# First feed-forward product in token-major form, seven products for eight in two of its k pairs

## The chip, the cores and the metric

The kernel runs on one core of a Trainium2 chip. The metric is device time in microseconds, from three timed runs; one further execution was taken with the hardware profiler, and all rows come from that one.

## What is computed

One decoder layer for 256 tokens of width 2048, all in float32. The change concerns the second half, the gated feed-forward block:

```python
x = layer_norm(ALPHA * x + merged @ w_o, ln1_g, ln1_b)
gate_f, up = split(x @ w_ffn_in, 2)            # 2048 -> 2 x 5632
f = (silu(gate_f) * up) @ w_ffn_out            # 5632 -> 2048
x = layer_norm(ALPHA * x + f, ln2_g, ln2_b)
```

Ahead of it stand the combined input projection with attention, a gated spatial mixing and a state-space layer (S5), which the change only touches at two small places.

## The kernel before

**Precision.** Every weight and activation is cut into a high part (float32r, by a copy on ScalarE) and a low part (the remainder, by a subtraction on VectorE). A product is high x high + high x low + low x high.

**Units.** All weights stream through units of up to 128 x 1024 elements (512 KB). A unit is loaded on SP's DMA queue into one of four raw buffers (`raw`), copied (`split_h`, line 263), subtracted (`split_l`, line 269) into one of four pairs `wh`, `wl`, and consumed by TensorE. The order on every engine is the program's own: the loop over the units calls `advance` (copies for units up to three ahead, as long as fewer than four pairs are live; loads as long as a raw buffer is free), emits the unit's matmuls, one step of each spawned task (generators that `yield` between units), the unit's `post`, deferred work (`later`), and then `remainders` (the subtractions, each followed by the next load).

**First product (`wide`).** An item is one 128-column tile of the gate or of the up matrix, k = 2048, in two units of eight k tiles. The weights are stationary, the activations move: line 80 takes the high weights over 512 columns (256 tokens high, 256 low), line 81 the low weights over the 256 high columns. The two halves of the PSUM bank are added in `sum_halves`; a gate tile becomes tanh(x/2), an up tile completes silu(gate) x up, and `copy_split` writes the high and low part of the feature-major h tile. There are 88 items; the first four run through `quad_tiles`, the others one after another.

**Second product (`tall`).** Token-major: activations stationary, weights moving with 512 columns, three matmuls per k tile and token half (lines 166 to 168). Its first unit's `before`, `ln2_load`, loads the second norm's weights into the buffer of the activations `x1T`.

**Residual.** `z` (256 x 2048, the first norm's result in rows) stays in SBUF, in the buffer with the tag t16, from the first norm to the end.

**S5.** `s5_setup` and `tables` are tasks in the first 60 us or so; GpSimd then runs a recurrence of 128 steps (lines 547 to 550), whose result TensorE reads in `s5_out` (line 561).

## Time and profile before

| | |
|---|---|
| time, median of 3 runs | 1589.97 us (1588.33 to 1590.55) |
| profiled execution, own time | 1590.49 us |
| its span, first to last instruction | 1588.7 us |
| TensorE busy | 1566.2 us, 99% |
| VectorE / ScalarE / GpSimd busy | 59% / 48% / 35% |
| DMA | 307.5 MB, 194 GB/s |

A busy time counts an instruction from start to end, and matmuls overlap: a matmul is busy for longer than the distance to the next one (its pitch). Costs on TensorE are therefore read as distances between starts.

### The profile page before, as it was taken

The numbers are of one execution on the slowest core, as the hardware profiler recorded it, in microseconds if no ns is written. First come the engines' busy times: TensorE is split into PE (matmuls) and PEld (weight loads), VectorE is DVE, ScalarE is ACT, GpSimd is POOL, SyncE is SP. The second block draws the span as 40 slices with busy tenths as digits, with TensorE's granted clock in tenths as the row PEclk, the third lists the DMA queues.
The fourth block names the chain that finished last, engine by engine and source line by source line (L and its number), as shares of the span: only waits on it lengthen the run. The fifth ranks groups of instructions, "written<-read, shape, count | busy, mean of one in ns | idle before, by whom it ended". The sixth has DMA issues, their size and how long they took to land.

```text
span 1588.7 us, 24112 instructions
## 1 busy us (share of the span) xinstructions
PE 1566.2 (99%) x9094; PEld 1359.8 (86%) x9094; DVE 931.2 (59%) x1232; ACT 762.9 (48%) x1040; POOL 557.8 (35%) x1147
## 2 busy tenths in 40 slices
PE   8999999999999999999999999999999999999996
PEld 6888888998889998889789888888888888888885
DVE  5545555656755665469667555555555555455455
ACT  5444444556544444465444545454545444443342
POOL 7469999944999999103011000000000000000002
PEclk9999999999999999999999999999999999999998
DMA  8575566665656555557863555555555556666663
GB/s 276 178 249 187 190 210 191 181 179 175 214 185 197 183 185 194 178 161 207 296 225 121 190 192 182 190 184 188 184 188 184 187 186 232 218 191 195 195 191 105
DMA packets 106492, 307.50 MB, mean 194 GB/s; under 512 B 27567, under 2 KB 28079, under 8 KB 106120
## 3 DMA queue, kind: packets, MB, share of 16 engines
q1 hardware_dynamic: 106280, 305.82, 60.0%
q8 instruction: 71, 1.16, 0.3%
q14 instruction: 45, 0.37, 0.1%
q0 software_dynamic: 96, 0.15, 0.0%
HBM read 303.78 MB, written 5.53 MB: 195 GB/s over the span
## 4 chain that ended last, share of the span: by engine, by line
PE 94%; DVE 3%; DMA 1%; ACT 1%; issue 1%; POOL 0%; SPq 0%; POOLq 0%; ACTq 0%
PE ps_mm L80 40%; PE ps_mm L81 20%; PE ps_mm L166 9%; PE ps_mm L167 9%; PE ps_mm L168 9%; DVE wl L269 2%; PE ps_mm L868 1%; PE ps_mm L867 1%; PE ps_mm L866 1%; PE ps_sd L525 1%; PE ps_mm L109 0%; PE ps_mm L112 0%; PE ps_sd L670 0%; DMA raw<-in_w_o_dram 0%; PE ps_sd L719 0%
## 5 line engine op out<-in xcount | busy, mean ns | idle before, releaser
L269 DVE TENSOR_TENSOR wl<-raw,wh 128x1024 fp32r<-128x1024 f32 (+1 forms) x544 | 654.3, 1227 | 157.5 <-ACT wh L263 156.8
L263 ACT ACTIVATE wh<-raw 128x1024 fp32r<-128x1024 f32 (+1 forms) x544 | 556.7, 1024 | 371.0 <-PE ps_mm L168 169.1
L80 PE MATMUL ps_mm<-xT,wh 128*128 128x512 f32 x1344 | 482.6, 402 | 7.5 <-ACT wh L59 5.5
L80 PE MATMUL ps_mm<-x1T,wh 128*128 128x512 f32 x1344 | 474.9, 399 | 0.0
L81 PE MATMUL ps_mm<-xT,wl 128*128 128x256 f32 x1344 | 379.8, 283 | 0.4 <-DVE wl L269 0.4
L81 PE MATMUL ps_mm<-x1T,wl 128*128 128x256 f32 x1344 | 378.0, 281 | 0.0
L80 PEld LDWEIGHTS ps_mm<-xT,wh 128*128 128x128 f32 x1344 | 254.7, 190 | 69.5 <-ACT wh L59 5.5
L80 PEld LDWEIGHTS ps_mm<-x1T,wh 128*128 128x128 f32 x1344 | 252.9, 188 | 62.7
L947 POOL TENSOR_TENSOR z<-z,ln2w 128x512 f32<-128x512 f32 (+1 forms) x4 | 5.2, 1302 | 726.6 <-ACT z L946 726.6
L81 PEld LDWEIGHTS ps_mm<-xT,wl 128*128 128x128 f32 x1344 | 256.8, 191 | 1.2 <-DVE wl L269 0.7
L81 PEld LDWEIGHTS ps_mm<-x1T,wl 128*128 128x128 f32 x1344 | 254.5, 189 | 0.0
L547 POOL TENSOR_TENSOR t<-s5keep,X 128x48 f32<-128x48 f32 x254 | 132.3, 521 | 44.2 <-ACT X L529 24.4
L550 POOL TENSOR_TENSOR X<-X,t 128x48 f32<-128x48 f32 x255 | 129.0, 506 | 20.0
L167 PE MATMUL ps_mm<-wl,h 128*128 128x512 f32 x340 | 132.5, 390 | 0.0
L166 PE MATMUL ps_mm<-wh,h 128*128 128x512 f32 x340 | 132.4, 390 | 0.0
L168 PE MATMUL ps_mm<-wh,h 128*128 128x512 f32 x340 | 132.4, 390 | 0.0
L549 POOL TENSOR_TENSOR X<-X,t 128x48 f32<-128x48 f32 x255 | 115.0, 451 | 40.5 <-ACT X L529 40.5
L1047 DVE TENSOR_TENSOR tmp<-ps_mm,tmp 128x256 f32<-128x256 f32 x88 | 37.4, 425 | 153.1 <-ACT tmp L1046 153.1
L548 POOL TENSOR_TENSOR t<-s5keep,X 128x48 f32<-128x48 f32 x254 | 116.4, 458 | 0.0
L318 ACT ACTIVATE tmp<-ps_mm,bcol 128x256 f32<-128x256 f32 x90 | 42.6, 473 | 136.7 <-PE ps_mm L81 136.5
L1046 ACT ACTIVATE tmp<-ps_mm 128x256 f32<-128x256 f32 x88 | 33.6, 382 | 152.0 <-PE ps_mm L81 152.0
L166 PEld LDWEIGHTS ps_mm<-wh,h 128*128 128x128 f32 x340 | 63.9, 188 | 13.3
(214 smaller groups left out, 1758.2 us busy)
## 6 DMA issues: line engine op xcount, KB each, us to landing
raw<-in_w_f_dram SPq DMA_DIRECT2D x264, 512.0 KB, 4.1
raw<-in_w_b_dram SPq DMA_DIRECT2D x164, 512.0 KB, 4.7
raw<-in_w_o_dram SPq DMA_DIRECT2D x32, 512.0 KB, 5.1
raw<-in_w_v_dram SPq DMA_DIRECT2D x24, 512.0 KB, 4.0
raw<-in_w_p_dram SPq DMA_DIRECT2D x32, 384.0 KB, 3.6
raw<-in_w_zv_dram SPq DMA_DIRECT2D x16, 384.0 KB, 3.7
tmp<-tab SPq DMA_DIRECT2D x64, 64.0 KB, 2.8
raw<-in_w_p_dram SPq DMA_DIRECT2D x16, 256.0 KB, 2.9
```

The costliest lines, as they stand in the source:

```text
L80: T.matmul(ps, lhsT=h[:, j * 128:(j + 1) * 128], rhs=a, start=k == 0, stop=last, skip_group_check=True)
L81: T.matmul(ps[:, 0:256], lhsT=l[:, j * 128:(j + 1) * 128], rhs=a[:, 0:256], start=False, stop=last, skip_group_check=True)
L166: T.matmul(ps[:, :n], lhsT=ah, rhs=hs, start=k == 0, stop=False)
L167: T.matmul(ps[:, :n], lhsT=ah, rhs=ls, start=False, stop=False)
L168: T.matmul(ps[:, :n], lhsT=al, rhs=hs, start=False, stop=k == total - 1)
L263: A.activation(h[:, :m], raws[n][:, :m], AF.Copy)
L269: V.tensor_tensor(l[:, :m], raws.pop(n)[:, :m], h[:, :m].bitcast(F32), op=ALU.subtract)
L318: A.activation(t, ps[:, 256:512], AF.Identity, bias=bcol[:, col:col + 1], scale=scale)
L547: G.tensor_tensor(t1, keep[:, 0], prev, op=ALU.mult)
L548: G.tensor_tensor(t2, keep[:, 1], prev[:, :, ::-1], op=ALU.mult)
L549: G.tensor_tensor(cur, cur, t1, op=ALU.add)
L550: G.tensor_tensor(cur, cur, t2, op=ALU.add)
```

## The change

For ten groups of four column tiles (all but the first group) the first product is now token-major: the activations are stationary and 512 weight columns (four tiles side by side) move. A unit is one pair of k tiles for the four gate tiles or the four up tiles, loaded as 512 runs of 1 KB where it was 128 runs of 4 KB. A group has eight k pairs. In six of them a gate and an up unit each take 12 matmuls (`mk8`). In the pairs 3 and 5 the 2 x 2 blocks (two token halves, two k tiles; two k tiles, gate and up) are multiplied with seven products for eight: `combine` forms sums of weights on VectorE before the split, four units `g`, `u`, `t1`, `tt` take 6, 6, 3 and 6 matmuls, and the sums of activations `S` are formed once (`sums`). Eight PSUM banks hold a group; `evict`, `gates_` and `ups` add them up, and `turns` transposes the gated product into the feature-major h tiles, during the group behind.

`S` lies in the buffer t16; so `first_sums` writes the residual rows to DRAM (GpSimd's queue) and `ln2_load` reads them back. In the early part, `s5_setup` waits three units longer before its transposes, and `tables` pauses after each of its four blocks.

```diff
+    PAIRS = (3, 5)
+    SP = len(PAIRS)
+    FIRST, LAST = 1, 10
...
         def load(n):
             u = units[n]
+            if u.role in ("t1", "tt"):
+                return
             r = raw_tile()
-            nc.sync.dma_start(r[:, :u.k * u.n], u.src)
+            if u.role:
+                u.pair[u.role] = r
+            dst = r[:, :u.k * u.n]
+            nc.sync.dma_start(dst if len(u.src.shape) == 2 else dst.rearrange("p (f c) -> p f c", f=u.src.shape[1]),
+                              u.src)
             raws[n] = r
...
+            if u.role == "g" and "t" not in u.pair:
+                combine(u.pair)
+            elif u.role == "t1":
+                raws[n] = u.pair["t"][:, 0:512]
+            elif u.role == "tt":
+                raws[n] = u.pair["t"][:, 512:1536]
             A.activation(h[:, :m], raws[n][:, :m], AF.Copy)
             hl[n] = rest[n] = (h, l)
 
+        def combine(p):
+
+
+            p["t"] = s6([128, 1536], F32, "tt")
+            b = [p[e][:, 0:1024].rearrange("p (f k c) -> p k f c", f=4, k=2) for e in "gu"]
+            b11, b21, b12, b22 = b[0][:, 0], b[0][:, 1], b[1][:, 0], b[1][:, 1]
+            t1, t2, t4 = (p["t"][:, 512 * i:512 * i + 512].rearrange("p (f c) -> p f c", f=4) for i in range(3))
+            V.tensor_tensor(t1, b12, b11, op=ALU.subtract)
+            V.tensor_tensor(b12, b22, b12, op=ALU.subtract)
+            V.tensor_tensor(t2, b12, b11, op=ALU.add)
+            V.tensor_tensor(t4, b21, t2, op=ALU.subtract)
+
         def split_l(n):
-            m = units[n].k * units[n].n
+            u = units[n]
+            m = u.k * u.n
             h, l = rest.pop(n)
             V.tensor_tensor(l[:, :m], raws.pop(n)[:, :m], h[:, :m].bitcast(F32), op=ALU.subtract)
+            if u.role not in ("t1", "tt"):
+                pos["raw"] -= 1
+            if u.role is None and u.pair and "u" in u.pair:
+                combine(u.pair)
 
...
-            for _ in range(5):
+            for _ in range(8):
...
                 else:
                     V.tensor_copy(tb2, ps[0:8, 0:127])
+                yield
...
+        def first_sums():
+
+            big["zd"] = dram.tile([128, 2, D], F32, name="zd")
+            for t in range(2):
+                nc.gpsimd.dma_start(big["zd"][:, t, :], big["z"][:, t, :])
+            spawn(sums())
...
+            xr = s6([128, 4, 256], F32, "xr")
+            for i, e in enumerate(PAIRS):
+                x = big["x1T"][:, 2 * e:2 * e + 2, :].bitcast(F32)
+                V.tensor_tensor(xr[:, 2 * i:2 * i + 2], x[:, :, 0:256], x[:, :, 256:512], op=ALU.add)
...
+            V.tensor_tensor(sr[:, 0], a21, a22, op=ALU.add)
+            V.tensor_tensor(sr[:, 1], sr[:, 0], a11, op=ALU.subtract)
+            V.tensor_tensor(sr[:, 2], a11, a21, op=ALU.subtract)
+            V.tensor_tensor(sr[:, 3], a12, sr[:, 1], op=ALU.subtract)
...
+            big["S"] = sb.tile([128, 4, SP, 256], F32R, tag="t16", bufs=1, name="S")
+            for s in range(4):
+                o = big["S"][:, s]
+                copy_split(o[:, :, 0:128], o[:, :, 128:256], sr[:, s])
...
+        def three(ps, a, h, l, start, stop):
+            T.matmul(ps, lhsT=a[0], rhs=h, start=start, stop=False)
+            T.matmul(ps, lhsT=a[1], rhs=h, start=False, stop=False)
+            T.matmul(ps, lhsT=a[0], rhs=l, start=False, stop=stop)
...
+            def cols(w, j):
+                return w.rearrange("p (f k c) -> p k f c", f=4, k=2)[:, j]
+
+            def prod(n, a, h, l, start, stop):
+                if n not in P:
+                    P[n] = bank(tags[n in (1, 5, 6, 7)])
+                three(P[n], a, h, l, start, stop)
...
+            def mk(role, i):
+                def mm(h, l):
+                    z = 2 * PAIRS[i]
+                    ends = i == 0, i == SP - 1
+                    if role == "g":
+                        prod(1, act2(0, z), cols(h, 0), cols(l, 0), *ends)
+                        prod(2, act2(0, z + 1), cols(h, 1), cols(l, 1), False, False)
+                    elif role == "u":
+                        prod(7, act_s(2, i), cols(h, 0), cols(l, 0), *ends)
+                        prod(3, act_s(3, i), cols(h, 1), cols(l, 1), False, False)
+                    elif role == "t1":
+                        prod(5, act_s(0, i), h[:, 0:512], l[:, 0:512], *ends)
+                    else:
+                        prod(6, act_s(1, i), h[:, 0:512], l[:, 0:512], *ends)
+                        prod(4, act2(1, z + 1), h[:, 512:1024], l[:, 512:1024], False, False)
+                return mm
+
+            def mk8(up, i):
+                def mm(h, l):
+                    for t in range(2):
+                        for j in range(2):
+                            prod(((2, 4), (3, 8))[up][t], act2(t, 2 * i + j), cols(h, j), cols(l, j),
+                                 (i, j) == (0, 0), (i, j) == (7, 1))
+                return mm
...
+            def begin():
+                if g > FIRST:
+                    spawn(turns(g - 1))
+
+            def evict():
+                c = P["c"] = {n: tmp() for n in (1, 7, 6, 5)}
+                A.activation(c[1], P[1], AF.Copy)
+                V.tensor_tensor(c[6], P[6], c[1], op=ALU.add)
+                V.tensor_tensor(c[7], P[7], c[6], op=ALU.add)
+                V.tensor_tensor(c[6], P[5], c[6], op=ALU.add)
+                V.tensor_tensor(c[5], P[5], c[7], op=ALU.add)
+
+            def gates_():
+                c = P["c"]
+                P["w"] = [tmp(), tmp()]
+                for t, (n, m) in enumerate(((1, 2), (7, 4))):
+                    V.tensor_tensor(c[n], P[m], c[n], op=ALU.add)
+                    A.activation(P["w"][t], c[n], AF.Tanh, scale=0.5)
...
+            def ups():
+                c = P["c"]
+                for n, m in ((6, 3), (5, 8)):
+                    V.tensor_tensor(c[n], P[m], c[n], op=ALU.add)
+
+                def rest(t):
+                    w, a, b = P["w"][t], c[(1, 7)[t]], c[(6, 5)[t]]
+                    V.scalar_tensor_tensor(w, w, 1.0, a, op0=ALU.add, op1=ALU.mult)
+                    V.tensor_tensor(w, w, b, op=ALU.mult)
+                    if t == 0:
+                        later(lambda: rest(1), 0)
+                later(lambda: rest(0), 0)
+                big["w", g] = P["w"]
...
+            src = [d["w_f1"][8 * g + up:8 * g + 8:2].rearrange("f p k c -> p f k c") for up in range(2)]
...
+            for i in range(8):
+                s = [a[:, :, 2 * i:2 * i + 2, :].rearrange("p f k c -> p f (k c)") for a in src]
+                if i in PAIRS:
+                    e = PAIRS.index(i)
+                    pair = pairs[e]
+                    units.append(Unit(s[0], 8, 128, mk("g", e), role="g", pair=pair))
+                    units.append(Unit(s[1], 8, 128, mk("u", e), role="u", pair=pair))
+                    units.append(Unit(None, 4, 128, mk("t1", e), role="t1", pair=pair))
+                    units.append(Unit(None, 8, 128, mk("tt", e), role="tt", pair=pair,
+                                      post=evict if e == SP - 1 else None))
+                else:
+                    units.append(Unit(s[0], 8, 128, mk8(0, i), post=gates_ if i == 7 else None,
+                                      before=begin if i == 0 else None))
+                    units.append(Unit(s[1], 8, 128, mk8(1, i), post=ups if i == 7 else None,
+                                      pair=pairs[PAIRS.index(i + 1)] if i + 1 in PAIRS else None))
...
+        def turns(g):
+
+            tag = "mm" if (LAST - g) % 2 else "sd"
+            for _ in range(3):
+                yield
+            for t in range(2):
+                ps = bank(tag)
+                for f in range(4):
+                    T.transpose(ps[:, f * 128:(f + 1) * 128], big["w", g][t][:, f * 128:(f + 1) * 128], ident)
+                f = 4 * g
+                while f < 4 * g + 4:
+                    n = min(4 * g + 4, 12 if f < 12 else f + 3 - f % 3) - f
+                    h_tile(f)
+                    y = big["h0"][:, f:f + n] if f < 12 else big["h", (f - 12) // 3][:, f % 3:f % 3 + n]
+                    copy_split(y[:, :, t * 128:(t + 1) * 128], y[:, :, 256 + t * 128:256 + (t + 1) * 128],
+                               ps.rearrange("p (f c) -> p f c", f=4)[:, f - 4 * g:f - 4 * g + n], 0.5)
+                    f += n
+                yield
...
+            big["z"] = sb.tile([128, 2, D], F32, tag="t16", bufs=1, name="z")
+            for t in range(2):
+                nc.sync.dma_start(big["z"][:, t, :], big["zd"][:, t, :])
             w = sb.tile([128, 2, D], F32, tag="t32", bufs=1, name="ln2w")
+            spawn(turns(LAST))
             for i, nm in enumerate(("ln2_g", "ln2_b")):
                 nc.sync.dma_start(w[:, i, :], d[nm].partition_broadcast(128))
...
+            if 4 <= i < 8 * FIRST:
+                wide(srcs, 8, act_x1, post, before=first_sums if i == 4 else None)
+        for g in range(FIRST, LAST + 1):
+            seven(g)
+        for i, (srcs, post) in enumerate(f1):
+            if i >= 8 * LAST + 8:
```

TensorE in the first product. Before, the end of one item's tile and the start of the next (each half-item's `wh` serves eight such pairs):

```order
L80 MATMUL ps_mm_10333<-x1T_8812,wh_10279 128x512
L81 MATMUL ps_mm_10333<-x1T_8812,wl_10280 128x256
L80 MATMUL ps_mm_10384<-x1T_8812,wh_10302 128x512 [waits Activation_49]
L81 MATMUL ps_mm_10384<-x1T_8812,wl_10303 128x256 [waits DVE_49]
L80 MATMUL ps_mm_10384<-x1T_8812,wh_10302 128x512
```

Now, the units u, t1 and the first half of tt of a pair (the four outputs are the products 7, 3, 5 and 6):

```order
L1144 MATMUL ps_sd_11129<-wh_11072,S_9471 128x512 [waits Activation_49]
L1145 MATMUL ps_sd_11129<-wh_11072,S_9471 128x512
L1146 MATMUL ps_sd_11129<-wl_11073,S_9471 128x512 [waits DVE_49]
L1144 MATMUL ps_mm_11004<-wh_11072,S_9471 128x512
L1145 MATMUL ps_mm_11004<-wh_11072,S_9471 128x512
L1146 MATMUL ps_mm_11004<-wl_11073,S_9471 128x512
L1144 MATMUL ps_sd_11142<-wh_11099,S_9471 128x512 [waits PE_49,Activation_49]
L1145 MATMUL ps_sd_11142<-wh_11099,S_9471 128x512
L1146 MATMUL ps_sd_11142<-wl_11100,S_9471 128x512 [waits DVE_49]
L1144 MATMUL ps_sd_11157<-wh_11115,S_9471 128x512 [waits Activation_49]
L1145 MATMUL ps_sd_11157<-wh_11115,S_9471 128x512
L1146 MATMUL ps_sd_11157<-wl_11116,S_9471 128x512 [waits DVE_49]
```

A unit's low part is first read by its third matmul, where it was read by the second; a unit lasts 3 to 12 matmuls, where it lasted 16.

VectorE in the first product. Before, one up item, its two splits, and the gate item behind it (lines 1047, 1056, 1060 and 63 are the `post`):

```order
L1047 TENSOR_TENSOR tmp1_12521<-ps_mm_12482,tmp1_12521 128x256
L1060 TENSOR_TENSOR tmp1_12473<-tmp1_12473,tmp1_12521 128x256
L63 SCALAR_TENSOR_TENSOR h6_12320<-tmp1_12473,h6_12320 128x256
L269 TENSOR_TENSOR wl_12503<-raw_12426,wh_12502 128x1024
L269 TENSOR_TENSOR wl_12531<-raw_12449,wh_12530 128x1024
L1047 TENSOR_TENSOR tmp1_12572<-ps_mm_12533,tmp1_12572 128x256
L1056 SCALAR_TENSOR_TENSOR tmp1_12575<-tmp1_12575,tmp1_12572 128x256
```

Now, from the last units of a group (line 1213 and 1214 are its gated product) to the first pair of the next, with its combination (lines 290 to 293), one turn (line 66) and the pair's gate unit:

```order
L1213 SCALAR_TENSOR_TENSOR tmp2_10592<-tmp2_10592,tmp2_10529 128x512
L1214 TENSOR_TENSOR tmp2_10592<-tmp2_10592,tmp2_10531 128x512
L299 TENSOR_TENSOR wl_10623<-raw_10556,wh_10622 128x1024
L299 TENSOR_TENSOR wl_10645<-raw_10574,wh_10644 128x1024
L299 TENSOR_TENSOR wl_10665<-raw_10598,wh_10664 128x1024
L290 TENSOR_TENSOR tt_10680<-raw_10642,raw_10620 128x512
L291 TENSOR_TENSOR raw_10642<-raw_10642 128x4x128
L292 TENSOR_TENSOR tt_10680<-raw_10642,raw_10620 128x512
L293 TENSOR_TENSOR tt_10680<-raw_10620,tt_10680 128x512
L66 SCALAR_TENSOR_TENSOR h0_10707<-ps_mm_10702,h0_10707 128x3x128
L66 SCALAR_TENSOR_TENSOR h1_10710<-ps_mm_10702,h1_10710 128x128
L299 TENSOR_TENSOR wl_10688<-raw_10620,wh_10687 128x1024
```

The combination reads the two raw tiles of its pair (10620 and 10642) and stands ahead of their splits; the raw buffers are freed by the rows of line 299.

SP at the start of the second product. Before, the load of a unit, the second norm's weights, and the next loads:

```order
L252 DMA raw_13626<-in_w_f2_dram 128x1024
L252 DMA raw_13654<-in_w_f2_dram 128x1024
L1088 DMA ln2w_13659<-in_ln2_g_dram 128x2048
L1088 DMA ln2w_13659<-in_ln2_b_dram 128x2048
L252 DMA raw_13677<-in_w_f2_dram 128x1024
L252 DMA raw_13695<-in_w_f2_dram 128x1024
```

Now:

```order
L262 DMA raw_13093<-in_w_f2_dram 128x1024
L262 DMA raw_13115<-in_w_f2_dram 128x1024
L1280 DMA z_13120<-zd_9367 128x2048 x2
L1284 DMA ln2w_13123<-in_ln2_g_dram 128x2048
L1284 DMA ln2w_13123<-in_ln2_b_dram 128x2048
L262 DMA raw_13143<-in_w_f2_dram 128x1024
```

Two transfers of 1 MB stand ahead of the two that were there, and in front of the next weight load.

## Rows read from the trace of the kernel before

**Rows 1.** The page, engines: busy us, share of the span, instructions.
```profile
PE 1566.2 (99%) x9094; PEld 1359.8 (86%) x9094; DVE 931.2 (59%) x1232; ACT 762.9 (48%) x1040; POOL 557.8 (35%) x1147
```

**Rows 2.** TensorE's waits: waiting line, awaited line, total us, times, longest us.
```profile
PE ps_mm L80 <- ACT wh L59: 5.5, 1, 5.5
PE ps_mm L80 <- DVE xT L61: 2.0, 1, 2.0
PE ps_mm L167 <- DVE wl L269: 0.8, 1, 0.8
```

**Rows 3.** Busy us by stretch (first, second product), then granted clock, DMA share, GB/s.
```profile
988.00:1032.00 44.00, 44.00 (x251) 38.24 (x250) 25.85 (x35) 21.31 (x32) 0.00 (x0) 1.00 0.57 189
1384.00:1428.00 44.00, 44.00 (x196) 36.47 (x195) 22.61 (x21) 16.98 (x16) 0.00 (x0) 1.00 0.63 196
```

**Rows 4.** Timeline of TensorE in the first product: start us, busy us, line, shapes.
```profile
1000.03 0.40 PE L80 MATMUL ps_mm<-x1T,wh 128*128 128x512 f32 x1
...
1011.69 0.40 PE L80 MATMUL ps_mm<-x1T,wh 128*128 128x512 f32 x1
```

**Rows 5.** Timeline of TensorE in the second product.
```profile
1399.64 0.39 PE L166 MATMUL ps_mm<-wh,h 128*128 128x512 f32 x1
...
1403.95 0.39 PE L167 MATMUL ps_mm<-wl,h 128*128 128x512 f32 x1
```

**Rows 6.** Groups of matmuls by form: count, busy us, mean ns of one.
```profile
L109 PE MATMUL ps_mm<-x1T,wh 128*128 128x256 f32 x64 | 12.0, 285 | 0.0
L866 PE MATMUL ps_mm<-yc,wh 128*128 128x256 f32 x96 | 27.2, 284 | 0.0
```

**Rows 7.** Timeline of TensorE around four transposes (line 966).
```profile
829.56 0.39 PE L168 MATMUL ps_mm<-wh,m 128*128 128x512 f32 x1
829.79 0.60 PE L966 MATMUL ps_sd<-ident,z 128*128 128x128 f32 x4
830.14 0.48 PE L166 MATMUL ps_mm<-wh,m 128*128 128x512 f32 x1
830.46 0.40 PE L167 MATMUL ps_mm<-wl,m 128*128 128x512 f32 x1
```

**Rows 8.** VectorE and ScalarE: one timeline row, then groups by form.
```profile
1004.01 2.35 DVE L269 TENSOR_TENSOR wl<-raw,wh 128x1024 fp32r<-128x1024 f32 x2
...
L891 DVE SCALAR_TENSOR_TENSOR z<-z,ps_mm 128x512 f32<-128x512 f32 x7 | 4.8, 688 | 12.0 <-PE ps_mm L168 12.0
L942 DVE SCALAR_TENSOR_TENSOR tmp<-z,mv,ln2w 128x512 f32<-128x512 f32 x2 | 1.5, 744 | 0.0
...
L263 ACT ACTIVATE wh<-raw 128x1024 fp32r<-128x1024 f32 x169 | 178.0, 1054 | 23.1 <-PE ps_mm L80 21.0
L59 ACT ACTIVATE x1T<-ps_sd 128x512 fp32r<-128x512 f32 x8 | 4.8, 596 | 11.0 <-PE ps_sd L966 11.0
```

**Rows 9.** Loads (900 to 1300 us; 256-byte runs): issue ns, landing us; their stretch.
```profile
L252 SPq DMA_DIRECT2D raw<-in_w_f_dram x141: 327/328/328, 903.5 to 1299.3; - x141
DMA to landing us min/median/max: 3.5/4.0/5.2
...
L654 SPq DMA_DIRECT2D tmp<-tab x64: 573/614/1757, 261.2 to 331.0; - x64
DMA to landing us min/median/max: 2.4/2.8/4.4
...
261.20:271.70 10.50, 10.50 (x73) 9.01 (x72) 6.26 (x14) 5.06 (x8) 9.56 (x25) 1.00 0.64 137
```

**Rows 10.** The same view by stretch, at the start of the second product.
```profile
1339.70:1353.00 13.30, 13.30 (x61) 11.01 (x60) 6.35 (x6) 5.01 (x6) 0.00 (x0) 1.00 0.89 355
```

**Rows 11.** GpSimd's recurrence up to 340 us; TensorE's first reading of it.
```profile
L550 POOL TENSOR_TENSOR X<-X,t x127: 310/322/1375, 91.0 to 334.6; 128x48 f32<-128x48 f32 x127
...
L561 PE MATMUL ps_sd<-X,cm x96: 272/273/298, 343.6 to 348.6; 128*32 128x128 f32 x96
```

More of the change, by code (lines that the diff above doesn't have):

```diff
@@ L66, in hybrid_layer, with __init__ @@
     class Unit:
-        def __init__(self, src, k, n, mm, post=None, before=None, uses=1, home=None, fence=False):
+        def __init__(self, src, k, n, mm, post=None, before=None, uses=1, home=None, fence=False,
+                     role=None, pair=None):
             self.src, self.k, self.n = src, k, n
+            self.role, self.pair = role, pair
             self.mm, self.post, self.before = mm, post, before
@@ L287, in top_up @@
             seq = pos["seq"]
-            if pos["load"] < len(seq) and pos["load"] - pos["l"] < RAW_BUFS:
+            if pos["load"] < len(seq):
+                u = units[seq[pos["load"]][0]]
+                if u.role not in ("t1", "tt"):
+                    if pos["raw"] >= RAW_BUFS:
+                        return False
+                    pos["raw"] += 1
                 load(seq[pos["load"]][0])
@@ L1036, in h_tile @@
             i = (f - 12) // 3
-            if (f - 12) % 3 == 0 and ("h", i) not in big:
+            if ("h", i) not in big:
                 big["h", i] = s6([128, 3, 512], F32R, f"h{i}")
@@ L1063, in post_f1, with sums @@
             return post
+        def first_sums():
[3 more added lines that the diff above has]
+            spawn(sums())
+        def sums():
+            xr = s6([128, 4, 256], F32, "xr")
[3 more added lines that the diff above has]
+            yield
+            sr = s6([128, 4, 2, 128], F32, "sr")
+            a = xr.rearrange("p (i k) (t c) -> p k t i c", k=2, t=2)
+            a11, a21, a12, a22 = a[:, 0, 0], a[:, 0, 1], a[:, 1, 0], a[:, 1, 1]
+            V.tensor_tensor(sr[:, 0], a21, a22, op=ALU.add)
+            V.tensor_tensor(sr[:, 1], sr[:, 0], a11, op=ALU.subtract)
+            V.tensor_tensor(sr[:, 2], a11, a21, op=ALU.subtract)
+            V.tensor_tensor(sr[:, 3], a12, sr[:, 1], op=ALU.subtract)
+            for _ in range(2):
+                yield
[3 more added lines that the diff above has]
+                copy_split(o[:, :, 0:128], o[:, :, 128:256], sr[:, s])
+                if s % 2:
+                    yield
@@ new lines, in seven @@
+        def seven(g):
+            P = {}
+            tags = ("mm", "sd") if (LAST - g) % 2 else ("sd", "mm")
+            def cols(w, j):
[56 more added lines that the diff above has]
+            src = [d["w_f1"][8 * g + up:8 * g + 8:2].rearrange("f p k c -> p f k c") for up in range(2)]
+            pairs = [{} for _ in PAIRS]
+            for i in range(8):
[13 more added lines that the diff above has]
+                                      pair=pairs[PAIRS.index(i + 1)] if i + 1 in PAIRS else None))
@@ L1215, in hybrid_layer @@
             seq.insert(at + i, (first + i, at))
-        pos.update(load=4, h=4, l=4, live=4, seq=seq)
+        pos.update(load=4, h=4, l=4, live=4, raw=0, seq=seq)
         while top_up():
```

12 lines of the change are left out of this document (10 added, 2 removed).

## The prediction

> **What bounds the kernel now.** I read the engines' shares first, then who waits for whom, then the stretches of the two feed-forward products, then single instructions. TensorE is busy for 99% of the span [rows 1], and in all its waits are five, 9.0 us together: 5.5 and 2.0 us for the first splits of weights and x, and three of at most 0.8 us [rows 2]. So no engine off TensorE costs anything now, and nothing can be gained by relieving one: below, every cost that is not a TensorE instruction has nothing as its lower bound. In the first product VectorE is busy for 25.85 of 44 us and ScalarE for 21.31, at a granted clock of 1.00, the 2.4 GHz level [rows 3]. The time is TensorE's instructions times their pitch, and the change must be counted in these.
>
> **TensorE, before.** In the first product one k tile of one column tile is a matmul of 512 moving columns and one of 256. From the start at 1000.03 to that at 1011.69 are 33 such pairs [rows 4]: 0.3533 us each. An item (one gate or up tile) has 16: 5.653 us. The ten groups replace 80 items: 1280 pairs x 0.3533 = **452.3 us**.
>
> **TensorE, after.** The token-major form is in the trace already, in the second product: three matmuls of 512 columns per k tile and token half, activations stationary. From 1399.64 to 1403.95 are 19 starts [rows 5]: 0.2268 us each. A group in that form without the seven products needs 192 of them, 43.5 us against 45.2 for eight items; over ten groups 435.5 us, a gain of 16.8 us from the form alone. In the two k pairs of a group 21 matmuls stand for 24, so a group has 186: 60 fewer in all, 13.6 us more. Together 1860 x 0.2268 = **421.9 us**, 30.4 us less.
>
> The moving operand is now four runs of 128 columns. Two runs of 128 in one operand took 285 ns of busy time where one run of 256 took 284 [rows 6]. I take nothing; one more ns per run, four per matmul, would be 7 us.
>
> The gated product now comes out token-major and is turned: 8 transposes in each group. Four of them stand in the trace in the middle of such matmuls: from the start at 829.79 to the second matmul after them, 830.46, is 0.67 us, where one matmul step is 0.227 [rows 7]: 0.443 us for four. Twenty fours: **8.9 us** (7.0 if only start to start, 0.35 us, counts; 12 by their busy time of 0.60).
>
> TensorE alone: 452.3 - 421.9 - 8.9 = **21.5 us less**.
>
> A rule on the pitch speaks against it. The rows give 0.2268 us for a matmul of 512 columns at 2.4 GHz and 0.3533 for the 512 and 256 together. The Trainium skill, "TensorE: Matmul & The Clock Gate", section "Wait — 56ns, not 53.3ns?", says that back-to-back matmuls start N ÷ 2.4 GHz + about 2.5 ns apart (215.7 ns measured for 512 columns). By that page, as an estimate, the pair is 324.9 ns, the form brings 1.8 us and not 16.8, the 60 matmuls 12.9 us, and the whole change 5.8 us before any stall. The trace disagrees with the page, by 5% for 512 columns and 9% for the pair; the measurement decides.
>
> **VectorE and ScalarE in a group.** A group now lasts 186 x 0.2268 + 0.89 = 43.07 us on TensorE. VectorE has 18 subtractions over 1024 columns, 1.175 us each (two in 2.35), and 24 operations over 512 columns (8 combine weights, 2 subtractions, 4 evict, 4 on gates and ups, 4 for the gated product, 2 after the turn); the nearest rows are 688 ns from PSUM and 744 in SBUF [rows 8]. 18 x 1.175 + 24 x 0.69 = 37.7 us, with the upper prices (1.22 and 0.75) 40.0. So VectorE goes from 59% of the stretch to 88%, at most 93%, and keeps 5.4 us, at least 3.1. ScalarE: 18 x 1.05 and 7 x about 0.6 [rows 8], 23 us, 54%.
>
> On average that fits. Two places are dense. First the weight buffers: a split may begin when TensorE has left the unit four back, and the units of a pair are short (6, 6, 3 and 6 matmuls). For the unit behind a pair the window is 15 matmuls, 3.4 us, and 0.45 us more since the low part is read only by the third matmul; the tail of the last matmul, 0.16 (busy for 0.39 us at a pitch of 0.227 [rows 5]), the copy on ScalarE, 1.05, and the subtraction, 1.2, are 2.4. It holds by 1.4 us. Behind the eviction four operations, 2.8 us, stand ahead of the next subtraction, in a window of two units, 5.4 us: 0.2 + 0.6 + 2.8 + 1.2 = 4.8, 1.0 us to spare with the low part's 0.45. Nothing is lost here, narrowly.
>
> Second, the **loads**. There are four raw buffers, and a combination needs both units of its pair, raw, before either is split. The up load of the first pair goes into the buffer that VectorE frees two subtractions (2.35 us) ahead of the combination; the up load of the second pair into one freed by the first pair's up unit, four subtractions (4.2 us) ahead. With d us from issue to landing VectorE stands still for d - 2.35 and d - 4.2 us. Loads of this stretch land after 3.5 to 5.2, median 4.0 us [rows 9]; these have 128 runs of 4 KB, the new ones 512 of 1 KB. The nearest row with many short runs: 64 KB in 256 runs of 256 bytes, issued in 573 ns or more against 328, landed after 2.4 to 4.4, median 2.8 us. If 128 more runs cost 0.25 us of issue, 384 more cost 0.75. Transport: 137 GB/s at a DMA share of 0.64, 214 at full share, while these 256-byte runs went, against 189 at 0.57, 332, for 4 KB [rows 3, 9]; 512 KB takes 2.45 us at the one and 1.6 at the other. So d lies between 4.0 and 5.6; I take 4.5, nearer the lower end, because the DMA engines have 43% of this stretch free and the load with 256 runs landed no later than those with 128. Then VectorE loses 2.15 + 0.3 = 2.4 of its 5.4 us: hidden, but barely, since it must also wait for TensorE at each group's end. At d = 5 it loses 3.5 us, and there I put the edge; beyond it each further us of d costs 2 to 3 us per group, 20 to 30 us in all. Cost: nothing to 18 us (at 5.6); I take **2.5**.
>
> **The small terms.** The residual rows go to DRAM and back, 1 MB per half. Out, they share the DMA with the weights while ScalarE, three units (8.5 us) after the issue, waits to write the sums into their buffer, and with it the splits behind: nothing to 2 us, once; 0.5. Back, 2 MB go ahead of the 2 MB of the last norm's weights on SP's queue, and the next weight loads stand behind both. In the trace this stretch moved 355 GB/s [rows 10], so 2 MB are 5.9 us more for a load that TensorE needs some 19 us after its issue; ScalarE and VectorE take 2.5 of these: nothing to 3 us; 1. The state-space setup is put back three units (8.5 us): GpSimd's first chain, whose last row starts at 334.6, would then end at 343.4, and TensorE asks for it at 343.6 [rows 11]. Nothing to 1.5 us; 0.3. All other sums (the activations' combinations, 6 operations and 8 splits once) lie in stretches where VectorE is idle for 40%.
>
> **The sum.** -21.5 + 2.5 + 0.5 + 1 + 0.3 = **-17.2 us**. The profiled execution took 1590.49 us, 1588.7 of it the span; this gives 1573.3. The median of the three runs is 0.5 lower: **1572.8 us**.
>
> **The rivals.**
> 1. The loads give part of it back (d from 5.0 to 5.7, or VectorE at its upper prices with d of 4.5 to 5.2). For it: two waits per group in one loop, VectorE at 88%, a run length that this trace shows in no load. Against: the queue moves 189 GB/s at a share of 0.57, so it isn't short of bandwidth. 7 to 14 us come back beyond the 2.5 taken: 1577 to 1586.
> 2. Slower: the combination becomes the bound. Its place is VectorE's first operation of each pair, its price 20 to 30 us per us of d beyond 5.0. From d = 5.9 the whole gain is spent; at 6.4 it is 1.4 x 25 = 35 us: 1590 - 21.5 + 1.8 + 35 = 1605. Against: the latest of 141 loads in this stretch landed after 5.2 us [rows 9].
> 3. The token-major form brings nothing: a 512-column matmul here starts after two thirds of a pair, 0.2355 us, and not 0.2268, as it would if the 4% between the forms lay in the stretch (its loads, its neighbours on the other engines) and not in the instructions. The 16.8 us go, the 60 matmuls give 14.1, the transposes cost 8.9: 1590 - 5.2 + 1.8 = 1587. Against: 33 pairs and 19 matmuls at one granted clock. The Trainium skill's rule of "TensorE: Matmul & The Clock Gate", above, would end beside it, at an estimated 1586.
> 4. The four-run operand or the transposes are dearer, by 4 to 10 us: 1576 to 1582.
>
> **How the numbers follow.** The forecast (1566 to 1576: no stall at all with the cheapest transposes, to twice the stall that I take) has 60%; rival 1 18%; rival 2 with d beyond 5.7 14%, of it 5% within 0.2%; rival 3 3%; rival 4 5%. A measurement of this kernel tells about 0.2% from no change, so faster means below 1586.8 us: 60 + 18 + 5 = 83%. Within 0.2%: 5 + 3 = 8%. Slower: 9%. The range from 1566 to 1586 leaves out rivals 2 and 3 and a little below: under 2 in 10.
>
> **What would show it.** Right: pitches of 0.227 us for 1860 matmuls; 43.1 us from one group to the next; TensorE without waits in the groups; VectorE near 88% there; loads landing at 4.3 to 4.8 us. Wrong at the loads: landings beyond 5 us, VectorE idle before the first operation of the combination, and TensorE waiting for the subtraction of the second pair's gate weights and of the unit behind the eviction. Wrong at the pitch: TensorE without waits, but groups longer than 43.1 us. The small terms show as single TensorE waits near 344 us, near the first eight items' end, and at the start of the second product.

## The result, and the profile after

The changed kernel takes **1573.72 us** (median; 1571.26 to 1574.72), the kernel before 1589.75 beside it: a ratio of 0.990, 95% interval 0.988 to 0.992. The forecast was 1572.8. The profiled execution took 1573.56 us, its span 1571.8, 16.9 less than before.

The answer to [rows 1] and [rows 2], the page's engines and TensorE's waits of the changed kernel (waiting line, awaited line, total us, times, longest):

```profile
PE 1546.5 (98%) x8474; PEld 1322.4 (84%) x8474; DVE 1034.5 (66%) x1318; ACT 767.6 (49%) x990; POOL 560.8 (36%) x1149
```

```profile
PE ps_mm L85 <- ACT wh L62: 5.7, 1, 5.7
PE ps_mm L172 <- DVE wl L299: 2.8, 2, 2.2
PE ps_mm L85 <- DVE xT L64: 2.0, 1, 2.0
PE ps_mm L86 <- DVE wl L299: 0.9, 2, 0.5
PE ps_mm L171 <- ACT wh L280: 0.4, 1, 0.4
```

TensorE is still the bound, and the groups' lines (L1144 to L1146) are in no row: no matmul is listed as waiting there. What is new is L172 and L171, at the second product's start. (Lines 80/81 are now 85/86, 166 to 168 are 171 to 173, 263 is 280, 269 is 299, 252 is 262.)

Where the time went shows in the first and last starts of three groups of matmuls: the second product's in the kernel before,

```profile
L166 PE MATMUL ps_mm<-wh,h x340: 388/390/395, 1335.7 to 1574.4; 128*128 128x512 f32 x170
```

and the groups' first and the second product's in the changed one.

```profile
L1144 PE MATMUL ps_mm<-wh,x1T x270: 389/389/476, 883.8 to 1299.0; 128*128 128x512 f32 x135
...
L171 PE MATMUL ps_mm<-wh,h x340: 387/389/494, 1314.7 to 1557.6; 128*128 128x512 f32 x170
```

Before, the 80 items ran for 452.3 us up to 1335.7, so from 883.4; now the ten groups run from 883.8 to 1314.7, 430.9 us. The rest of the span (second product and norm) was 1588.7 - 1335.7 = 253.0 us and is 1571.8 - 1314.7 = 257.1. So: 0.4 lost up to the groups, 21.4 gained in them, 4.1 lost behind them, together 16.9.

The stretches of two groups, from one eviction to the next (busy us by engine, then granted clock, DMA share and GB/s, as in [rows 3]):

```profile
915.00:958.20 43.20, 43.20 (x196) 35.75 (x195) 36.89 (x43) 22.71 (x27) 0.00 (x0) 1.00 0.63 195
958.20:1001.40 43.20, 43.20 (x196) 35.62 (x195) 36.27 (x43) 21.96 (x26) 0.00 (x0) 1.00 0.63 192
```

A group takes 43.20 us (43.07 forecast) with TensorE busy throughout; VectorE is busy for 36.6 of them, 85% (37.7 and 88% forecast).

### The profile page after: what moved, and what is told of

It reads as the page before. It is cut to its first block, busy times and chain, and to the rows that moved or that the text cites. A ratio compares the mean times of both kernels' runs of the same rounds, so it can differ in the third digit from the quotient of the medians.

```text
span 1571.8 us, 23107 instructions
## 1 busy us (share of the span) xinstructions
PE 1546.5 (98%) x8474; PEld 1322.4 (84%) x8474; DVE 1034.5 (66%) x1318; ACT 767.6 (49%) x990; POOL 560.8 (36%) x1149
## 4 chain that ended last, share of the span: by engine, by line
PE 91%; DVE 4%; DMA 2%; ACT 1%; issue 1%; POOL 0%; SPq 0%; POOLq 0%; ACTq 0%; DVEq 0%
PE ps_mm L85 21%; PE ps_mm L86 11%; PE ps_mm L171 8%; PE ps_mm L172 8%; PE ps_mm L173 8%; PE ps_sd L1146 5%; PE ps_sd L1144 4%; PE ps_mm L1144 4%; PE ps_mm L1146 4%; PE ps_sd L1145 4%; PE ps_mm L1145 4%; DVE wl L299 2%; PE ps_mm L908 1%; PE ps_mm L907 1%; PE ps_mm L906 1%; DMA raw<-in_w_f_dram 1%
## 5 line engine op out<-in xcount | busy, mean ns | idle before, releaser
L85 PEld LDWEIGHTS ps_mm<-xT,wh 128*128 128x128 f32 x1344 | 253.9, 189 | 70.3 <-ACT wh L62 5.7
L586 POOL TENSOR_TENSOR t<-s5keep,X 128x48 f32<-128x48 f32 x254 | 131.8, 519 | 50.7 <-ACT X L568 30.9
L589 POOL TENSOR_TENSOR X<-X,t 128x48 f32<-128x48 f32 x255 | 130.2, 511 | 20.0
L172 PE MATMUL ps_mm<-wl,h 128*128 128x512 f32 x340 | 132.4, 389 | 2.2 <-DVE wl L299 2.2
L171 PE MATMUL ps_mm<-wh,h 128*128 128x512 f32 x340 | 132.6, 390 | 0.4 <-ACT wh L280 0.4
L588 POOL TENSOR_TENSOR X<-X,t 128x48 f32<-128x48 f32 x255 | 119.3, 468 | 32.8 <-ACT X L568 32.8
L587 POOL TENSOR_TENSOR t<-s5keep,X 128x48 f32<-128x48 f32 x254 | 111.7, 440 | 0.0
L1144 PE MATMUL ps_sd<-wh,x1T 128*128 128x512 f32 x270 | 106.1, 393 | 0.0
L1144 PE MATMUL ps_mm<-wh,x1T 128*128 128x512 f32 x270 | 105.9, 392 | 0.0
L1146 PE MATMUL ps_sd<-wl,x1T 128*128 128x512 f32 x270 | 105.4, 390 | 0.0
L1146 PE MATMUL ps_mm<-wl,x1T 128*128 128x512 f32 x270 | 105.2, 390 | 0.0
L1145 PE MATMUL ps_mm<-wh,x1T 128*128 128x512 f32 x270 | 105.1, 389 | 0.0
L1145 PE MATMUL ps_sd<-wh,x1T 128*128 128x512 f32 x270 | 105.1, 389 | 0.0
L172 PEld LDWEIGHTS ps_mm<-wl,h 128*128 128x128 f32 x340 | 63.8, 188 | 15.6 <-DVE wl L299 2.6
```

The lines of the kernel that those rows point to most:

```text
L85: T.matmul(ps, lhsT=h[:, j * 128:(j + 1) * 128], rhs=a, start=k == 0, stop=last, skip_group_check=True)
L171: T.matmul(ps[:, :n], lhsT=ah, rhs=hs, start=k == 0, stop=False)
L172: T.matmul(ps[:, :n], lhsT=ah, rhs=ls, start=False, stop=False)
L586: G.tensor_tensor(t1, keep[:, 0], prev, op=ALU.mult)
L589: G.tensor_tensor(cur, cur, t2, op=ALU.add)
L1144: T.matmul(ps, lhsT=a[0], rhs=h, start=start, stop=False)
```

## Why VectorE's free time is not free

In the second of these groups, VectorE at its two combinations (timeline: start us, busy us, line, in brackets the idle time before and what ended it; rows between are left out at the dots):

```profile
980.38 0.69 DVE L290 TENSOR_TENSOR tt<-raw 128x512 f32<-128x512 f32 x1 [3.13 <-DMA raw<-in_w_f_dram]
...
992.98 0.69 DVE L290 TENSOR_TENSOR tt<-raw 128x512 f32<-128x512 f32 x1 [1.44 <-DMA raw<-in_w_f_dram]
...
995.15 0.69 DVE L293 TENSOR_TENSOR tt<-raw,tt 128x512 f32<-128x512 f32 x1
995.76 2.35 DVE L299 TENSOR_TENSOR wl<-raw,wh 128x1024 fp32r<-128x1024 f32 x2
```

and TensorE where it first reads what the last of these rows writes, the low part of the second pair's gate weights:

```profile
996.90 0.39 PE L1145 MATMUL ps_sd<-wh,x1T 128*128 128x512 f32 x1
997.13 0.40 PE L1146 MATMUL ps_sd<-wl,x1T 128*128 128x512 f32 x1
```

The first of the two subtractions ends at 995.76 + 1.2 = 996.97, the matmul starts at 997.13: 0.15 us to spare in this group. Elsewhere two weight loads of this line (TensorE's loading of its stationary operand) already wait for VectorE, 0.6 us together, without a matmul being listed as held up. All loads of the groups (line 262, 900 to 1300 us: issue ns, then issue to landing), and below them the one issued at 986.8, which ends the second wait:

```profile
L262 SPq DMA_DIRECT2D raw<-in_w_f_dram x149: 367/368/373, 899.8 to 1299.5; - x149
...
DMA to landing us min/median/max: 3.9/4.4/6.1
```

```profile
L262 SPq DMA_DIRECT2D raw<-in_w_f_dram x1: 368/368/368, 986.8 to 986.8; - x1
...
DMA to landing us min/median/max: 6.1/6.1/6.1
```

The median lies in the forecast's 4.3 to 4.8 (4.5 was taken), but the two loads on which the combinations hang are late ones in this group: 5.4 us for the first (issued at 975.0, the first of three within 2.3 us) and 6.1 for the second. The runs below tell whether this matters.

## Experiments

Theory: the gain is TensorE's instructions (form, 60 matmuls, turns); loads and combinations hide behind it; the second product's start loses some 2.6 us. Rivals: VectorE's loop already costs time, the form brings nothing, the turns are dearer. All times are medians, beside the changed kernel's 1573.7.

### The form without the seven products

```diff
-    PAIRS = (3, 5)
+    PAIRS = ()
...
-                    V.tensor_tensor(c[n], P[m], c[n], op=ALU.add)
-                    A.activation(P["w"][t], c[n], AF.Tanh, scale=0.5)
+                    A.activation(P["w"][t], P[m], AF.Tanh, scale=0.5)
```

> All eight k pairs of each group as eight products for eight: the token-major form, the turns and the short-run loads stay; the seven products, the weight combinations, the activation sums and the residual rows' way through DRAM go. Theory (TensorE's instructions alone set the time, 0.2268 us per 512-column matmul): 60 matmuls more than the changed kernel, +13.6, without the waits at the second product's start and for the sums' buffer, -3.1: 1584 us, that is 6 below the kernel before, from -16.8 for the form and +8.9 for the turns, rest in the odd waits. Group to group 192 x 0.2268 + 0.89 = 44.4 us. Rival of the page's pitch (the form brings 1.8 us and not 16.8): 1597 us. Rival that the seven products' gain is partly eaten by VectorE in the changed kernel: the difference to the changed kernel is above 12 us by that part, 1586 to 1590.

Measured: 1582.84 us (1581.97 to 1584.38; ratio to before 0.996, 0.995 to 0.997). From group to group, by the transposes' weight loads into one bank set (first start: the first turn of a group; last start: the second turn, eight groups later), in this kernel and in the changed one:

```profile
L1237 PEld LDWEIGHTS ps_mm<-ident,tmp x40: 140/140/140, 938.7 to 1298.4; 128*128 128x128 f32 x40
```

```profile
L1246 PEld LDWEIGHTS ps_mm<-ident,tmp x40: 140/140/140, 936.7 to 1285.9; 128*128 128x128 f32 x40
```

359.7 against 349.2 us: from a group's first turn to its second are 3.2 us in both, so the difference is that of eight groups, 1.31 us each for six matmuls, 0.219 for one (1.36 expected for six). Form and turns together bring 6.4 us, where the forecast's prices give 16.8 - 8.9 = 7.9: the form brings 15.3 if the turns cost 8.9. At the rival's pitch this kernel would be slower than the one before.

### One pair of the two

```diff
-    PAIRS = (3, 5)
+    PAIRS = (5,)
```

> Only one of the eight k pairs (the sixth) in seven products. Theory (each pair is worth 3 of 192 matmuls in each group, 0.68 us, and VectorE's combinations are wholly hidden): 30 matmuls more, +6.8, 1580.5 us, group to group 42.4 + 0.89 + ... = 43.75 us. Rival (the second pair's combination costs VectorE waits that TensorE feels, so the second pair brings less than the first): 1574 to 1578.

Measured: 1579.11 us (1576.99 to 1580.01), 5.4 above the changed kernel. That is 1.4 less than expected; the median lies outside the rival's 1574 to 1578, the range reaches into it, so the time alone doesn't part the two. The groups do (ScalarE's first eviction, eight groups apart; the changed kernel's 345.7 us by the same row stand below):

```profile
L1193 ACT ACTIVATE tmp<-ps_sd x5: 575/578/578, 912.6 to 1263.2; 128x512 f32<-128x512 f32 x5
```

350.6 against 345.7 us are 0.61 a group for the second pair's three matmuls, and 1.31 - 0.61 = 0.70 for the first's (0.68 expected for each). Each pair brings about half, and VectorE's second combination takes at most 0.1 us a group of it.

### The turns twice

```diff
-                for f in range(4):
+                for f in [*range(4), *range(4)]:
                     T.transpose(ps[:, f * 128:(f + 1) * 128], ...
```

> Each of the twenty sets of four transposes is issued twice into the same bank. Theory (four transposes among the matmuls cost TensorE 0.443 us): 20 x 0.443 = 8.9 us more, 1582.6 us; by start to start (0.35 us for four, once they stand in a row) 7.0 more, 1580.7; by their busy time (0.60) 12 more, 1585.7. Rival (the turns are hidden behind matmuls, or the group's end is set by another engine): no change, 1573.7.

Measured: 1578.22 us (1577.84 to 1580.7), only 4.5 more. Timeline of TensorE at a turn of this kernel:

```profile
935.25 1.04 PE L1246 MATMUL ps_mm<-ident,tmp 128*128 128x128 f32 x8
936.04 0.48 PE L1144 MATMUL ps_sd<-wh,x1T 128*128 128x512 f32 x1
936.36 0.40 PE L1145 MATMUL ps_sd<-wh,x1T 128*128 128x512 f32 x1
```

In the changed kernel the same turn starts at 936.90 and the second matmul behind it at 937.57, 0.67 us later, as in [rows 7]; with eight transposes it is 1.11, so four more cost 0.44 here. From group to group, by ScalarE's evictions of every second group (first and last start, eight groups apart), in the changed kernel and in this one:

```profile
L1193 ACT ACTIVATE tmp<-ps_mm x5: 578/581/582, 958.1 to 1303.8; 128x512 f32<-128x512 f32 x5
```

```profile
L1193 ACT ACTIVATE tmp<-ps_mm x5: 575/577/579, 957.3 to 1309.2; 128x512 f32<-128x512 f32 x5
```

345.7 against 351.9 us: 0.78 a group, 0.39 for each set of four, 7.8 us for twenty. The span rose by 4.3 only, to 1576.1. All of TensorE's waits in this profile are 8.8 us, where the changed kernel's five rows above have 11.8: 3.0 of the 3.5 that are missing. At the second product's start they fell from 2.6 to 0.8; that this follows from TensorE coming later wasn't tested. So the turns' price stands at 0.39 to 0.44 us for four; the total is no clean measure of it.

### Work added to VectorE

Two, then four operations more in each combination:

```diff
-            V.tensor_tensor(t4, b21, t2, op=ALU.subtract)
+            for _ in range(3):   # 5 in the second run
+                V.tensor_tensor(t4, b21, t2, op=ALU.subtract)
```

> The last operation of each weight combination is issued three times instead of once: 2 x 2 x 0.692 = 2.8 us more of VectorE per group. In the changed kernel VectorE is busy for 36.6 of 43.2 us per group and stands still for about 2.0 us more at the combination's loads. Theory (VectorE has 4.6 us to spare): 36.6 + 2.0 + 2.8 = 41.4 of 43.2, hidden, 1573.7 +- 1, no TensorE wait in the groups. Rival (VectorE is on the edge as the prediction put it, 3.0 us to spare, and its order in the group costs it more at the dense places): TensorE waits for the low parts behind the pairs, 0.5 to 2 us per group, 1579 to 1594.

> The same with four operations more per combination: 5.5 us more of VectorE per group. Theory (4.6 us to spare): 36.6 + 2.0 + 5.5 = 44.1 us against 43.2, VectorE becomes the bound, 0.9 us per group if the loads still cost it 2.0 us, 10 us in all, 1583; if its lateness lets the loads land in time (the 2.0 us go), it would stay hidden but for the dense places, 1574 to 1580. Rival (the prediction's edge, 3.0 us to spare): 2.5 us per group, 1599.

Measured: **1599.26** (1595.67 to 1599.64) and **1632.96** us (1627.68 to 1637.36), 25.5 and 59.2 more. Both rivals were too mild. The expectations also misread a number: VectorE's waits for loads are 2.0 us each, and there are two in a group, not one. With two operations more, VectorE's wait for the loads (900 to 1300 us), TensorE's waits in the groups and TensorE at the place shown above:

```profile
DVE tt L290 <- DMA raw<-in_w_f_dram: 33.4, 17, 3.1
```

```profile
PE ps_sd L1147 <- DVE wl L300: 9.0, 6, 2.6
PE ps_mm L1147 <- DVE wl L300: 8.5, 9, 1.6
```

```profile
996.04 0.39 PE L1146 MATMUL ps_sd<-wh,x1T 128*128 128x512 f32 x1
998.99 0.50 PE L1147 MATMUL ps_sd<-wl,x1T 128*128 128x512 f32 x1 [2.55 <-DVE wl L300]
```

VectorE's waits for loads are what they were (33.1 us in the same stretch of the changed kernel). They don't shrink when VectorE is late, since VectorE's own subtractions free the buffers that these loads need. All 149 loads of that stretch waited for them on SP's queue (changed kernel):

```profile
SPq L262 <- DVE wl L299: 334.9, 149, 7.8
```

So a late VectorE makes the loads late, its idle time is no reserve, and the second pair's gate weights take the delay at once. The first 1.38 us per combination cost 25.5 us, 18 for each us, against the 20 to 30 forecast for each us of landing. The next 1.38 cost 33.7, but not by this chain alone. In the first run the granted clock is 1.00 throughout the groups; in the second it falls behind TensorE's stops. One stop (timeline), the stretch behind it, and the groups as a whole (as in [rows 3]; the clock is the number after the last bracket):

```profile
961.77 0.79 PE L1147 MATMUL ps_mm<-wl,x1T 128*128 128x512 f32 x1 [3.05 <-DVE wl L300]
```

```profile
962.00:966.00 4.00, 4.00 (x10) 3.13 (x11) 3.77 (x4) 1.06 (x1) 0.00 (x0) 0.50 0.72 209
883.80:1366.00 482.20, 439.08 (x1884) 353.09 (x1882) 408.20 (x499) 219.57 (x255) 0.00 (x0) 0.97 0.55 169
```

0.50 is the lower of the clock's two levels, 1.2 GHz. 3% of 482 us is an estimate of up to 14 us for it, so the second step gives no price of the chain.

### Loads in long runs

```diff
-                s = [a[:, :, 2 * i:2 * i + 2, :].rearrange("p f k c -> p f (k c)") for a in src]
+                s = [d["w_f1g"][g, up, i] for up in range(2)]
```

Here w_f1g is a second copy of these weights, laid out by the host.

> The host lays the ten groups' weights out so that each 512 KB load has 128 runs of 4 KB, as the kernel before had, and not 512 of 1 KB; nothing else changes. Theory (the loads' wait, some 2 us in each group, is hidden behind TensorE): landings fall from 4.4 to about 4.0 us and the issue from 368 to 328 ns, VectorE's waits at the combination shrink by about 0.4 us each, the time stays, 1573.7 +- 1. Rival (the short runs cost TensorE something): up to 3 us less, 1571.

Measured: 1572.53 us (1570.85 to 1577.94), no difference that the runs can tell. Landing of the groups' loads, and VectorE's waits for them:

```profile
DMA to landing us min/median/max: 3.3/3.5/5.7
```

```profile
DVE tt L290 <- DMA raw<-in_w_f1g_dram: 12.4, 10, 1.5
```

The landing falls to 3.5 us, more than expected (4.0). The short runs cost 0.9 us of landing, and VectorE 21 us in 400; TensorE feels nothing that the runs can tell. Now the same with two operations more per combination:

> Two operations more per combination, as in the first run of that kind (1599.3 us, 25.5 above the changed kernel), but the ten groups' loads in 128 runs of 4 KB. Theory (TensorE waits for the low part of the second pair's gate weights, at the end of: buffer freed, load landed, combination, subtraction; the changed kernel meets it with 0.15 us to spare at a landing of 6.1 us, and the long runs bring that load 2.2 us earlier): the first two operations are within the spare time or 0.5 us over it, 1573 to 1580. Rival (VectorE's sum of work in the group is what counts, and the loads have no part in it): 25 us as before, 1598.

Measured: **1574.17** us (1573.62 to 1577.26) in place of 1599.26. So the loads are a link of the chain: with the landings shorter, the same added work is hidden nearly whole. VectorE's sum of work, the rival, has fallen for this amount of work.

### The gate's subtraction ahead of the combination

```diff
-            if u.role == "g" and "t" not in u.pair:
-                combine(u.pair)
...
-            if u.role is None and u.pair and "u" in u.pair:
+            if u.role == "g":
                 combine(u.pair)
```

With two operations more per combination:

> Two operations more per combination, loads in short runs as in the changed kernel, but VectorE subtracts the gate unit's low part ahead of the combination instead of behind it (the gate's split needs the gate's load alone). Theory (the chain over the second load and the combination to the gate's low part is what TensorE waits for; now the up unit's low part ends it, which TensorE asks for 1.4 us later): most of the 25.5 us go, 1574 to 1585. Rival (VectorE's sum of work counts, or the loads move later with the order): 1595 to 1600.

Measured: 1594.26 us (1589.97 to 1596.87): 5 of the 25.5 us back, not most; that is just below the rival's 1595 to 1600, and the theory has failed. The moved combination lets the turn's subtraction pass it, and that waits for TensorE's transposes:

```profile
981.00 0.69 DVE L66 SCALAR_TENSOR_TENSOR h<-ps_sd,h 128x512 fp32r<-128x512 f32 x1 [4.06 <-ACT h L62]
```

VectorE's waits for loads are nearly gone (2.3 us in 400), but it waits 36.6 us for the turns instead. The edit changed two things, so this run doesn't settle which chain is the tightest.

### Residual rows and norm weights later

```diff
-            for t in range(2):
-                nc.sync.dma_start(big["z"][:, t, :], big["zd"][:, t, :])
...
+        def late_load():
+            for _ in range(4):
+                yield
...
+            for t in range(2):
+                nc.sync.dma_start(big["z"][:, t, :], big["zd"][:, t, :])
+                for _ in range(4):
+                    yield
...
```

> In the second feed-forward product the residual rows come back from DRAM at its units 4 and 8 and the last norm's weights at units 12 and 16, one 1 MB transfer at a time, where the changed kernel issues all 4 MB ahead of its first unit. Theory (TensorE waited 2.6 us at this product's start, because the weight loads stood behind 4 MB on SP's queue): these waits go, 1571.1 us, 2.6 below the changed kernel's 1573.7, and the second product takes 240.3 us rather than 242.9. Rival (the waits come from VectorE and ScalarE, which are still busy with the last group's gated product and its turn): the waits stay, 1573.7 +- 0.5. A third outcome, the 1 MB transfers collide with the weight loads later: waits of 0.5 to 3 us in the middle of the product, 1573 to 1575.

Measured: **1570.14** us (1569.42 to 1570.85; ratio 0.988, 0.987 to 0.990), 3.6 below the changed kernel (2.6 expected): the fastest of all. At the start of the second product of the changed kernel, TensorE (timeline), the load that it waits for (the first behind the 4 MB), and ScalarE's copy of it:

```profile
1335.26 0.49 PE L171 MATMUL ps_mm<-wh,h 128*128 128x512 f32 x1 [0.39 <-ACT wh L280]
...
1338.00 0.50 PE L172 MATMUL ps_mm<-wl,h 128*128 128x512 f32 x1 [2.24 <-DVE wl L299]
```

```profile
L262 SPq DMA_DIRECT2D raw<-in_w_f_dram x1: 328/328/328, 1320.8 to 1320.8; - x1
...
DMA to landing us min/median/max: 13.3/13.3/13.3
```

```profile
1334.15 1.06 ACT L280 ACTIVATE wh<-raw 128x1024 fp32r<-128x1024 f32 x1 [6.68 <-DMA raw<-in_w_f_dram]
```

In the run with late transfers these waits are absent, and the second product's matmuls stand so:

```profile
L171 PE MATMUL ps_mm<-wh,h x340: 389/389/476, 1314.2 to 1553.9; 128*128 128x512 f32 x170
```

From there to the span's end, 1568.1, are 253.9 us: the 253.0 of before and 0.9 for two turns. So the 4 MB ahead of the weights cost 3.2 us.

### Three pairs, and all edits together

```diff
-    PAIRS = (3, 5)
+    PAIRS = (1, 3, 5)
```

> Three of the eight k pairs (the second, fourth and sixth) in seven products; the sums of the activations grow by half. TensorE: 30 matmuls fewer, 42.5 us per group, -6.8 in all. VectorE: four operations of 0.69 and subtractions of 0.68 and 1.22 more, 4.7 us, so 41.3 us busy; with the loads' waits of 2 us (two pairs) to 3 (three) 43.3 to 44.3. Theory (VectorE has 4.6 us to spare at two pairs and none at three): VectorE sets the pace at 43.3 to 44.3 us per group, +1 to +11 against the changed kernel, 1575 to 1585. Rival (the waits for loads only fill spare time and shrink when VectorE is late): the third pair brings most of its 6.8 us, 1567 to 1570.

Measured: 1623.38 us (1621.69 to 1625.63), 50 more, far beyond the expected 1 to 11. TensorE now also waits for the turn's subtraction, which still holds banks that the first pair's products need:

```profile
PE ps_mm L1144 <- DVE h L66: 9.0, 5, 1.9
PE ps_sd L1144 <- DVE h L66: 7.1, 4, 1.9
```

VectorE's waits for loads have shrunk here, as the rival had it (900 to 1300 us; 33.1 with two pairs), and TensorE is slower all the same. Part of that is the clock again: 0.98 from 883.8 to 1366 us, an estimate of up to 10 us.

```profile
DVE tt L290 <- DMA raw<-in_w_f_dram: 6.5, 9, 1.3
```

Then late transfers, long runs and the moved combination together, with two pairs, and with the third, fifth and seventh:

> Three edits together on the changed kernel: residual rows and norm weights late in the second product, long runs, the gate's subtraction ahead of the combination. Theory (the groups are at TensorE's instructions already, so two of the three only add spare time, and the first is worth 3 us): 1569 to 1570.5, TensorE without waits in groups and second product. Rival (single matmuls in the groups are held up by less than the profile lists as waits): 1565 to 1568.

> The same three edits with three pairs in seven products (the third, fifth and seventh). TensorE 6.8 us less. VectorE 41.3 of 42.5 us, of it 0.6 us or less left for waits at three loads and the banks. Theory (VectorE works in the loop with loads and banks that cost it 2 to 3 us a group): 43.3 to 44.3 us per group and more where the turn's banks are held, 1570 to 1590. Rival (with loads in time VectorE can run at 97%): 1563.

Measured: 1573.49 us (1572.22 to 1574.25) and 1573.49 (1572.11 to 1574.3). The first is 3.4 slower than the late transfers alone, against the expectation: the turn's subtraction is ahead of the combination again, and VectorE waits for it (first row, the kernel with two pairs); eight groups, from 955.7 to 1305.5 us, take 43.7 us each and not 43.2, and TensorE stands for 2.5 us in them (second row), all of it listed as waits for low parts. That the moved combination does this, and not the long runs beside the late transfers, is read from the trace; no run holds these two alone.

```profile
DVE h L66 <- ACT h L62: 41.7, 25, 4.1
```

```profile
955.70:1305.50 349.80, 347.32 (x1554) 285.01 (x1553) 294.55 (x351) 181.12 (x215) 0.00 (x0) 1.00 0.59 193
```

With three pairs the theory's 1570 to 1590 holds. The matmuls saved are lost again: VectorE is busy for 329.0 of 350 us, 94%, and waits for no load, so there its sum of work is nearly all that is left.

```profile
950.00:1300.00 350.00, 344.41 (x1534) 280.58 (x1533) 328.98 (x400) 190.89 (x232) 0.00 (x0) 1.00 0.60 193
```

## Why the prediction was right, step by step

- **TensorE's instructions: right.** Forecast for the groups' stretch, which holds 18 of the 20 turns: 421.9 + 8.0 = 429.9 us; measured 430.9, with no wait listed. The 1.0 us is about 0.1 in each group and isn't explained. The Trainium skill's rule in "TensorE: Matmul & The Clock Gate", section "Wait — 56ns, not 53.3ns?", was a rival here; it states 215.7 ns for a matmul of 512 columns. The trace disagrees with it as before: 43.20 us less 0.89 for the turns are 0.2275 us for each of 186 matmuls, and the run with the form alone bears the trace out.
- **The four-run operand: nothing, as taken.** 0.2275 us a matmul in the groups, 0.2268 in [rows 5]; all 0.13 us of a group's surplus would be 0.7 ns per matmul.
- **The turns: 0.443 us for four, confirmed** at 0.67 less 0.227 (0.39 by doubling them).
- **The loads: the waits were foreseen, their price was mis-sized.** The 2.5 us taken were not paid: the long runs gain nothing that can be told. The median landing, 4.4, was as forecast (the issue was dearer by 0.04 us, not 0.75), but the argument used it for the loads that count, which take 5.4 and 6.1 having been issued close behind others. By the forecast's edge (5.0, then 20 to 30 us for each us) that should have cost 8 us or more, and nothing shows of it. VectorE had 1.1 us less work in a group than forecast (36.6, not 37.7); whether that is all of the difference wasn't tested. The edge is where the kernel now stands, 0.15 us away in the group shown. "Hidden, but barely" was right, the 3 us to spare were not: the sum counted all idle time as reserve, while the runs with added work show that it is tied to the loads. Rivals 1 and 2 describe the mechanism, and the added work shows a price near theirs (18 us for each us). Rival 1's time is added up wrongly: 7 to 14 us beyond the 2.5 taken give 1580 to 1587, not 1577 to 1586.
- **Second product's start: mis-sized.** 1 us taken (0 to 3), 3.2 measured by moving the transfers. The step that failed is "a load that TensorE needs some 19 us after its issue": issued at 1320.8, it was needed at 1334.9 (1335.26 less the wait of 0.39), 14.1 us later. It landed after 13.3 us, 4.3 more than the load behind the 2 MB of the kernel before (issued at 1340.7, 9.0), where 5.9 were forecast. ScalarE and VectorE then took 3.9 us to the matmul that reads its low part (1338.00), not 2.5; the last group's turn stands between on both.
- **The other small terms:** 0.5 and 0.3 taken; the groups begin 0.4 us later than the items did, and no wait is listed near 344 us.

So the sum came to 0.3 us of the profiled gain (17.2 against 16.9) partly by luck: 2.5 us not paid at the loads and 0.4 at the other small terms, against 1.0 unexplained in the groups and 2.2 too little at the second product's start.

## What to carry to other kernels

When an engine waits for a load whose buffer it frees itself, its idle time can be part of a loop and no reserve: find the first consumer on the bound engine and read how many tenths of a us it has left. Size such a wait by the landing of the very load that ends it, not by the median of its line. Bulk transfers not needed for tens of us belong behind the loads that are due, one by one.

## What the runs showed of the hardware

A 512 KB load in 512 runs of 1 KB was issued in 368 ns and landed after 4.4 us, in 128 runs of 4 KB in 328 ns and 3.5, at 192 to 195 GB/s in either case. A VectorE operation of two operands over 512 columns took 0.68 to 0.69 us whether one operand came from PSUM or both from SBUF. Behind a stop of TensorE of 3.05 us, matmuls of 512 columns ran at a granted clock of 0.50: 10 of them were counted in 4 us, where at 1.00 one started every 0.2275 us.
